# A decoder block with an RWKV-7 mixer: the order of the A products of a pair of heads on TensorE

## The chip, the cores and the metric

The kernel runs on one core of a Trainium2 chip. The metric is the device time of one execution in microseconds (us). The kernel before took 3034.74 us in the median of three runs (3031.83 to 3035.33).

The engines are named as in the profile: PE is TensorE's matmul, PEld its weight load, DVE is VectorE, ACT is ScalarE, POOL is GpSimd, SP is SyncE, which issues most DMAs.

## The reference, cut to what matters

The input x has 2048 tokens of 1024 channels. It is normalised, modulated, and multiplied by one large matrix `w_in`. The columns feed two branches: a causal depthwise convolution of width 31 with gates, and an RWKV-7 token mixer with 16 heads of 64 channels. Both are projected, merged by sigmoid gates, projected again and added to x.

The change lies in the mixer. Its state is a 64 x 64 matrix for each head, updated token by token:

```python
def step(state, inp):
    r_t, w_t, k_t, v_t, kk_t, b_t = inp
    sk = jnp.einsum('bhvk,bhk->bhv', state, kk_t)
    state = (state * w_t[:, :, None, :] - sk[..., None] * b_t[:, :, None, :]
             + v_t[..., None] * k_t[:, :, None, :])
    return state, jnp.einsum('bhvk,bhk->bhv', state, r_t)
```

## The kernel before, in words

The kernel works on this recurrence in chunks of 64 tokens. Within a chunk the tokens' influence on each other is a matrix of inner products, called A here: the products of the two operand sets `BK` (keys and in-context-rate keys, divided by their decay) and `KR` (normalised keys and receptances, multiplied by their decay). From A the kernel then inverts a triangular system and passes the state from chunk to chunk.

The 2048 tokens are four blocks (`b`) of 512, each of `NCH` = 8 chunks. In a block the 16 heads are four groups (`g`), each of two pairs (`q`), each of two heads (`hh`). So there are 4 x 4 x 2 = 32 calls of `pair`. Head 0 of a pair has its 64 channels in partitions 0 to 63 of every tile of the pair, head 1 in partitions 64 to 127.

`pair` (from line 456) prepares one pair and stops at three `yield`s. The first part makes the decay factors (the scans of line 477, the exponentials of lines 480 and 482). The second makes `KR` and `BK`: two projections through `shifted`, the eight small matmuls of line 504 for the head norms, and the element-wise lines 511, 517 (`BK`) and 522 (`KR`). The third is the place of the change:

- Lines 527 to 539, the A products. `c4` counts the two halves of the pair's eight chunks. For each half there are two PSUM tiles `pA`, one for each head, and eight matmuls (line 534): four chunks `c` and two heads `hh`, the head innermost. A matmul contracts over the head's 64 partitions and writes 128 x 128 values: chunk `c` goes to a quarter of the head's tile. The four of one head form one group in one bank (`start` at `c == 0`, `stop` at `c == 3`). Then line 537 (DVE) reads each of the two tiles, multiplies by a mask and writes `Asb`.
- Line 543 multiplies triangular parts by the norms. Lines 546 to 559 make the values (`shifted`, transposes at line 550 into a PSUM tile `pv`, and the products of lines 286 and 287 into a PSUM tile `pb`). Line 562 (POOL) overwrites `BK` in place, once all products of it are done. Line 568 transposes it, line 569 copies it out.

All those PSUM tiles have the tag `aux` and come from one pool `pa` of `PAB` = 3 buffers. A tile's first writer waits until an earlier tile has given a buffer back, that is, until its last reader is done.

After both pairs, `group` runs the inversion (POOL, lines 623 to 628, then small matmuls of lines 657 and 666) and the chain over the eight chunks: line 684 (state times operands), DVE line 686, line 689, DVE line 691, line 695, DVE line 699. That chain of a group runs while the next group's pairs are prepared. The large projections of the convolution and the gates (`conv`, `gates`, through `project` and `mm3k`, line 206) are put between all this; there are three matmuls for each tile of weights, since each 32-bit operand is split into a high and a low part.

What order results: the kernel is written for a scheduler that runs at build time. It keeps a model of the engines' time, and at each step gives an engine the instruction of highest priority (the program's order, raised in places by `tc.high_priority`) whose operands and buffers its model has ready. The result is a fixed list for each engine. On the chip each engine works through its list in order. So a matmul of head 1 whose buffer the model does not have yet is passed by others that are ready.

One `nc.tensor.matmul` on 32-bit operands stands as two records in the trace, so one half of a pair is 16 records of line 534 and a pair is 32. The projections' operands (line 206) have one record each.

Of the kernel before, what the change touches and what calls it, by code (L numbers as in the profile page):

```python
# [81 lines left out]
def hybrid_block(ctx: ExitStack, tc: tile.TileContext, x, vecs, convk, w2a2, final_g, ada, w_in, w_co, w_ro, w_o, crow, out,  # L82
                 seq=2048, groups=(0, 1, 2, 3), phase2=True, dbg=None):
    nc = tc.nc
# [48 lines left out]
    def flat(ap):  # L133
        return ap.rearrange("p a b -> p (a b)")
# [321 lines left out]
    def pair(b, q_, pr, h, lora, uv, Asb, rn, res):  # L456
# [30 lines left out]
        KR = l3.tile([P, NCH // 2, 4 * CH], F32, name="KR", tag="KR", bufs=KRB)  # L487
        BK = l3.tile([P, NCH // 2, 4 * CH], F32, name="BK", tag="BK", bufs=BKB)
# [14 lines left out]
        for c in range(NCH):  # L503
            nc.tensor.matmul(pss[prow(c % 2), c // 2, :], sq[:, c * CH:c * CH + CH], hones, start=True, stop=True,
                             skip_group_check=True)
# [20 lines left out]

        for c4 in range(NCH // 4):
            pA = [pa.tile([P, 2, 256], F32, name="aux", tag="aux") for _ in range(2)]
            for c in range(4):
                cc, e = (c4 * 4 + c) // 2, c % 2  # L530
                es = slice(e * 128, e * 128 + 128)
                for hh in range(2):
                    hs = slice(64 * hh, 64 * hh + 64)
                    nc.tensor.matmul(pA[hh][:, c // 2, es], BK[hs, cc, es], KR[hs, cc, es],  # L534
                                     start=(c == 0), stop=(c == 3), skip_group_check=True)
            for hh in range(2):
                nc.vector.tensor_tensor(  # L537
                    out=Asb[:, hh, c4 * 4:c4 * 4 + 4, :].rearrange("p (a e) n -> p a (e n)", e=2),
                    in0=pA[hh], in1=flat(maskA).unsqueeze(1).broadcast_to([P, 2, 256]), op=ALU.mult)
# [24 lines left out]
        for c4 in range(NCH // 4):  # L564
            pt = pa.tile([P, 4, P], F32, name="aux", tag="aux")
            for c in range(4):
                cc, e = (c4 * 4 + c) // 2, c % 2
# [5 lines left out]
    def group(b, g, h, lora, fill):  # L573
        uv = l3.tile([P, NCH, 2, P], F32, name="uv", tag="uv", bufs=2)
        As = [l3.tile([P, 2, NCH, P], F32, name="As", tag="As", bufs=ASB) for _ in range(2)]
        R = [{}, {}]
        rn = lt.tile([P, 2, NCH // 2, 2], F32, name="rn", tag="rn")
        pairs = [pair(b, q, 2 * g + q, h, lora, uv, As[q], rn, R[q]) for q in range(2)]
        for i, q in enumerate(ORD):
            next(pairs[q])  # L580
# [589 lines left out]
```

## Time and profile before

| what | value |
|---|---|
| median of three runs | 3034.74 us |
| the profiled execution, whole time | 3047.45 us |
| its span, first to last instruction | 3045.7 us |
| granted TensorE clock, mean over the span | 0.975 |
| stage of the four blocks' mixers (line 534 runs from 89.4 to 2309.9 us) | 2221 us |
| what follows it to the end of the span, mostly the output projections | 736 us |

The profiled execution is 12.7 us (0.4%) above the median; sums are made against it and carried over to the median as they stand.

How to read the lines: a group's line has line, engine, operation, the tile written and the tiles read, the count after x, then busy time in us and mean ns of one, then the engine's idle time just before and what ended it. A line of the timeline has the start in us, the time from the first start to the last end in us, engine, line, operation, tiles, shape, count, and in brackets the idle time before it with its releaser. A matmul's time in such a line reaches to the end of its pipeline, so the next line can start before it. A line of windows has the stretch, its length, and for each engine busy time and count, then the granted clock, the share of the DMA engines and GB/s.

### The profile page before, as it was taken

What the parts mean: (1) busy time and instruction counts of PE and PEld (TensorE: products, weight loads), DVE (VectorE), ACT (ScalarE), POOL (GpSimd) and SP (SyncE); (2) the same over time, 40 slices, a digit from 0 to 9 for tenths busy, and PEclk for the clock granted to TensorE, in tenths of its full rate; (3) what the DMA queues carried; (4) which work ended last, traced back from release to release, by engine and by line L of the source; (5) the groups of instructions that cost most, each with busy time, mean ns of one, the idle gap of its engine ahead of it and who ended that gap; (6) DMA issues with size and microseconds to landing.
All of it is one profiled execution on the core that took longest, in us unless ns stands there. A gap on an engine that the chain in (4) does not pass through costs nothing.

```text
span 3045.7 us, 64763 instructions
## 1 busy us (share of the span) xinstructions
PE 2914.9 (96%) x25672; PEld 2735.9 (90%) x25672; DVE 2058.4 (68%) x3896; ACT 935.2 (31%) x1759; POOL 1250.1 (41%) x1786
## 2 busy tenths in 40 slices
PE   6999998999999999899999999999999999899998
PEld 6889998989989899899999999999999988788988
DVE  6587877686867676668676767676779635776433
ACT  4433434332323232233232323232323222333201
POOL 3455555434343425143434263625467204565000
PEclk9899999999999999999999999999999999999999
DMA  8666758564758578847474777655647778889674
GB/s 303 205 234 209 251 196 282 199 235 145 250 185 260 187 242 287 235 137 246 151 246 139 246 254 252 199 185 165 212 141 246 229 264 309 320 311 344 239 280 163
DMA packets 368673, 699.24 MB, mean 230 GB/s; under 512 B 136241, under 2 KB 154993, under 8 KB 368370
## 3 DMA queue, kind: packets, MB, share of 16 engines
q1 hardware_dynamic: 368370, 695.10, 68.0%
q8 instruction: 202, 3.31, 0.4%
q14 instruction: 101, 0.83, 0.1%
HBM read 506.14 MB, written 187.70 MB: 228 GB/s over the span
## 4 chain that ended last, share of the span: by engine, by line
PE 61%; DMA 16%; DVE 9%; POOL 7%; SPq 3%; issue 2%; ACT 2%; ACTq 0%; DVEq 0%; POOLq 0%
PE ps_main L206 43%; DMA w_st<-w_in_t 3%; PE aux L534 2%; POOL TT L627 2%; POOL itmp L625 2%; DMA w_st<-w_ro_t 2%; DMA w_st<-w_co_t 2%; PE pout L1091 2%; PE pout L1092 2%; PE pout L1090 2%; PE xo L689 2%; DVE acc L774 1%; DMA w_gr<-grow_d 1%; PE xo L684 1%; PE xo L695 1%
## 5 line engine op out<-in xcount | busy, mean ns | idle before, releaser
L206 PE MATMUL ps_main<-h_hi,w_hi 128*128 128x256 f32 x4608 | 971.3, 289 | 12.2 <-ACT w_hi L189 3.4
L206 PE MATMUL ps_main<-h_hi,w_lo 128*128 128x256 f32 x4608 | 965.4, 289 | 8.5 <-POOL w_lo L191 5.0
L206 PE MATMUL ps_main<-h_lo,w_hi 128*128 128x256 f32 x4608 | 971.3, 289 | 0.0
L206 PEld LDWEIGHTS ps_main<-h_hi,w_hi 128*128 128x128 f32 x4608 | 735.3, 194 | 24.1 <-ACT w_hi L189 3.9
L206 PEld LDWEIGHTS ps_main<-h_hi,w_lo 128*128 128x128 f32 x4608 | 731.8, 194 | 17.5 <-POOL w_lo L191 6.3
L206 PEld LDWEIGHTS ps_main<-h_lo,w_hi 128*128 128x128 f32 x4608 | 733.9, 194 | 8.1 <-issue 0.5
L774 DVE SCALAR_TENSOR_TENSOR acc<-u,ck,acc 128x512 f32<-128x512 f32 x928 | 698.6, 753 | 20.8
L625 POOL TENSOR_TENSOR itmp<-La,TT 128x126 f32<-128x126 f32 (+22 forms) x496 | 180.2, 363 | 140.9 <-DMA La<-dA 106.1
L627 POOL TENSOR_TENSOR TT<-TT,itmp 128x126 f32<-128x126 f32 (+22 forms) x496 | 188.2, 379 | 37.3
L681 ACT ACTIVATE Se<-S,pe 128x128 f32<-128x128 f32 x256 | 89.0, 395 | 239.4 <-DVE S L699 239.2
L191 POOL TENSOR_TENSOR w_lo<-w_st,w_hi 128x1024 fp32r<-128x1024 f32 x47 | 113.6, 2417 | 112.8 <-ACT w_hi L189 106.2
L699 DVE TENSOR_TENSOR S<-xo,Se 64x128 f32<-64x128 f32 x256 | 73.5, 287 | 104.1 <-PE xo L695 100.8
L189 ACT CAST w_hi<-w_st 128x1024 fp32r<-128x1024 f32 x71 | 74.2, 1046 | 182.4 <-DMA w_st<-w_in_t 147.4
L534 PE MATMUL aux<-KR,BK 64*128 64x128 f32 x1024 | 121.5, 307 | 7.4 <-POOL BK L517 4.1
L534 PEld LDWEIGHTS aux<-KR,BK 64*128 64x128 f32 x1024 | 104.2, 208 | 18.7 <-POOL BK L517 4.3
L562 POOL TENSOR_TENSOR BK<-BK,pe 128x1024 f32<-128x1024 f32 x32 | 62.0, 1939 | 140.7 <-PE aux L534 113.1
L691 DVE TENSOR_TENSOR uv<-xo,rn 64x256 f32<-64x256 f32 x128 | 53.8, 420 | 90.7 <-PE xo L689 88.8
L686 DVE TENSOR_TENSOR XO<-xo,XO 128x256 f32<-128x256 f32 x128 | 53.7, 420 | 89.9 <-PE xo L684 70.5
L537 DVE TENSOR_TENSOR As<-aux,maskA 128x512 f32<-128x512 f32 x128 | 83.8, 685 | 36.9 <-PE aux L534 35.6
L684 PE MATMUL xo<-S,KR 128*128 128x128 f32 x512 | 83.0, 285 | 15.0 <-DVE S L699 14.9
L786 ACT ACTIVATE th<-ps_main 128x512 f32<-128x512 f32 x64 | 38.1, 596 | 190.1 <-PE ps_main L206 168.9
L431 ACT ACTIVATE t<-ps_main,mu 128x512 f32<-128x512 f32 x96 | 65.6, 683 | 97.4 <-PE ps_main L206 90.4
(301 smaller groups left out, 5318.2 us busy)
## 6 DMA issues: line engine op xcount, KB each, us to landing
w_hi<-kh_in SPq DMA_DIRECT2D x219, 512.0 KB, 5.1
w_lo<-kl_in SPq DMA_DIRECT2D x219, 512.0 KB, 4.0
w_st<-w_in_t SPq DMA_DIRECT2D x73, 512.0 KB, 4.9
kh_in<-w_hi SPq DMA_DIRECT2D x71, 512.0 KB, 2.9
kl_in<-w_lo SPq DMA_DIRECT2D x71, 512.0 KB, 3.7
w_hi<-kh_ro SPq DMA_DIRECT2D x32, 512.0 KB, 5.6
w_lo<-kl_ro SPq DMA_DIRECT2D x32, 512.0 KB, 5.5
w_hi<-kh_co SPq DMA_DIRECT2D x32, 512.0 KB, 5.5
```

Of the source, the lines that this page charges most:

```text
L189: nc.scalar.copy(hi, st)
L191: lo_eng.tensor_tensor(out=lo, in0=st, in1=hi.bitcast(F32), op=ALU.subtract)
L206: nc.tensor.matmul(ps[:, qs], ww[:, k, :], aa[k][:, qs], start=(k == 0 and t == 0 and q == 0), stop=(k == KT - 1 and t == 2 and q == ms - ...
L431: nc.scalar.activation(t1, ps, AF.Identity, scale=mu1[:, mi:mi + 1])
L534: nc.tensor.matmul(pA[hh][:, c // 2, es], BK[hs, cc, es], KR[hs, cc, es], start=(c == 0), stop=(c == 3), skip_group_check=True)
L537: nc.vector.tensor_tensor(out=Asb[:, hh, c4 * 4:c4 * 4 + 4, :].rearrange("p (a e) n -> p a (e n)", e=2), in0=pA[hh], in1=flat(maskA).unsqu ...
L625: nc.gpsimd.tensor_tensor(out=tmp[:, :ni, :nt], in0=La[:, j:j + 1, j + 1:].broadcast_to([P, ni, nt]), in1=TT[:, :ni, j:j + 1].broadcast_to ...
L627: nc.gpsimd.tensor_tensor(out=TT[:, :ni, j + 1:], in0=TT[:, :ni, j + 1:], in1=tmp[:, :ni, :nt], op=ALU.add)
L681: nc.scalar.mul(Se[:, q, :], Sg[:, q, :], R[q]["pe"][:, c:c + 1])
L684: nc.tensor.matmul(xo[:, q, :], R[q]["KR"][:, cc, es], Sg[:, q, :], start=(q == 0), stop=(q == 1), skip_group_check=True)
L699: nc.vector.tensor_tensor(out=Sg[hs, :, hs], in0=xo[hs, 2:4, hs], in1=Se[hs, :, hs], op=ALU.add)
L774: nc.vector.scalar_tensor_tensor(out=acc if i + 1 < HALO else yj, in0=u[:, i:i + TB], scalar=ck[:, j, i:i + 1], in1=acc, op0=ALU.mult, op1 ...
```

## The change

The four chunks' matmuls move into a function `aprod(c, hh)`, which is the same matmul. The first product of head 0 is issued; the first product of head 1 is to stand behind it on TensorE; all six others are to stand behind that second one. `tc.issue_after(ins)` gives every instruction traced in its block an edge of order to `ins` on the same engine; it adds no instruction and no semaphore wait of its own. The set of matmuls, their operands, tiles and flags are the same, and so are the DVE operations and the pool.

```diff
         for c4 in range(NCH // 4):
             pA = [pa.tile([P, 2, 256], F32, name="aux", tag="aux") for _ in range(2)]
-            for c in range(4):
+
+            def aprod(c, hh):
                 cc, e = (c4 * 4 + c) // 2, c % 2
                 es = slice(e * 128, e * 128 + 128)
-                for hh in range(2):
-                    hs = slice(64 * hh, 64 * hh + 64)
-                    nc.tensor.matmul(pA[hh][:, c // 2, es], BK[hs, cc, es], KR[hs, cc, es],
-                                     start=(c == 0), stop=(c == 3), skip_group_check=True)
+                hs = slice(64 * hh, 64 * hh + 64)
+                return nc.tensor.matmul(pA[hh][:, c // 2, es], BK[hs, cc, es], KR[hs, cc, es],
+                                        start=(c == 0), stop=(c == 3), skip_group_check=True)
+
+            with tc.issue_after(aprod(0, 0).ins):
+                second = aprod(0, 1)
+            with tc.issue_after(second.ins):
+                for c in range(1, 4):
+                    for hh in range(2):
+                        aprod(c, hh)
```

## The prediction

> **What bounds the kernel now.** I read the page first: which engine is full, and what the products cost. Then the windows by stage, to see whether that holds where the products lie.
>
> ```profile
> span 3045.7 us, 64763 instructions
> PE 2914.9 (96%) x25672; PEld 2735.9 (90%) x25672; DVE 2058.4 (68%) x3896; ACT 935.2 (31%) x1759; POOL 1250.1 (41%) x1786
> ...
> PE 61%; DMA 16%; DVE 9%; POOL 7%; SPq 3%; issue 2%; ACT 2%; ACTq 0%; DVEq 0%; POOLq 0%
> ...
> L774 DVE SCALAR_TENSOR_TENSOR acc<-u,ck,acc 128x512 f32<-128x512 f32 x928 | 698.6, 753 | 20.8
> ...
> L534 PE MATMUL aux<-KR,BK 64*128 64x128 f32 x1024 | 121.5, 307 | 7.4 <-POOL BK L517 4.1
> ...
> L562 POOL TENSOR_TENSOR BK<-BK,pe 128x1024 f32<-128x1024 f32 x32 | 62.0, 1939 | 140.7 <-PE aux L534 113.1
> ...
> L537 DVE TENSOR_TENSOR As<-aux,maskA 128x512 f32<-128x512 f32 x128 | 83.8, 685 | 36.9 <-PE aux L534 35.6
> ```
> ```profile
> core 0: us, PE busy (x) PEld busy (x) DVE busy (x) ACT busy (x) POOL busy (x), PEclk, DMA share, GB/s
> 89.00:114.00 25.00, 21.63 (x127) 19.49 (x128) 20.23 (x39) 13.30 (x26) 10.29 (x9) 0.60 0.56 183
> 114.00:2310.00 2196.00, 2126.31 (x20491) 2036.12 (x20489) 1573.69 (x2896) 697.97 (x1286) 982.26 (x1535) 0.98 0.65 213
> ```
>
> TensorE is full over the stage where all but the first pair's products lie: 2126.31 of 2196 us, so 69.7 us idle, while DVE is at 72%. Of TensorE's time 121.5 us are the products, 1024 records, which is 32 pairs of 32 records. A busy TensorE is not one at its peak, so the question is how densely these records stand. The timeline of one ordinary pair shows it.
>
> ```profile
> 402.18 2.05 PE L534 MATMUL aux<-KR,BK 64*128 64x128 f32 x24
> 404.16 0.50 PE L206 MATMUL ps_main<-h_lo,w_hi 128*128 128x256 f32 x2
> ...
> 406.47 1.16 PE L534 MATMUL aux<-KR,BK 64*128 64x128 f32 x8
> 407.55 0.39 PE L206 MATMUL ps_main<-h_hi,w_lo 128*128 128x256 f32 x1
> ```
> ```profile
> 402.18:403.07 0.89, 0.89 (x16) 0.89 (x17) 1.00 0.00 0
> 406.47:407.36 0.89, 0.89 (x8) 0.89 (x8) 1.00 1.01 216
> ```
>
> The run of 24 is the first half (16 records, the heads by turns) and then head 0 of the second half alone (8); the run of 8 is head 1 of the second half, later. The two windows are cut at the starts of these runs: in 0.89 us stand 16 records where the heads alternate and 8 where one head stands alone. So a record costs 0.056 us by turns and 0.112 us alone: products on the two halves of the partitions run beside each other, products on the same half do not. The second half is torn apart because its head 0 finds the third `aux` buffer free, while head 1 needs one that DVE's line 537 gives back.
>
> **The change part by part.** *First half.* By turns already; nothing changes.
>
> *Second half, head 0.* A product is 2 x 0.112 = 0.223 us alone. From 402.18 to 404.16 the long run takes 1.98 us: 0.89 for the first half, 0.89 for head 0's four products, and 0.20 that is left, for the pipeline and the change to 128-row matmuls. After the change only head 0's first product can stand there, the other three are held behind head 1's first. The run becomes 0.89 + 0.22 + 0.20 = 1.31 us: 0.67 us less.
>
> *Second half, head 1.* The later run takes 407.55 - 406.47 = 1.08 us: 0.89 for four products and 0.19 at its end. After the change it has seven products: head 1's first beside head 0's second, and so on, and head 1's last alone. That is four steps of 0.223 us again, with head 0's three hidden beside head 1's: 1.08 us as before. No run is added.
>
> The sum over the pairs is 32 x 0.67 = 21.4 us at the full clock. TensorE is what is late in this stage, and the work that follows on its list (line 206 above) moves up by as much, so most of it reaches the end.
>
> *What of it is eaten by waits.* Where TensorE already waits between these two runs for something that does not move, the gain only lengthens the wait. Two pairs of that kind:
>
> ```profile
> 1018.25 2.05 PE L534 MATMUL aux<-KR,BK 64*128 64x128 f32 x24
> ...
> 1022.26 0.68 PE L684 MATMUL xo<-S,KR 128*128 128x128 f32 x4 [1.29 <-DVE S L699]
> ```
> ```profile
> 247.19 2.05 PE L534 MATMUL aux<-KR,BK 64*128 64x128 f32 x24
> ...
> 252.00 0.81 PE L684 MATMUL xo<-S,KR 128*128 128x128 f32 x4 [2.10 <-DVE S L699]
> ```
>
> Four of the 32 pairs have such a wait of 0.4 us or more there. Those 4 x 0.67 = 2.7 us I count as nothing: 18.7 us are left.
>
> *Half clock.* Some products run at half clock and would give twice as much:
>
> ```profile
> 1159.86 0.71 PE L689 MATMUL xo<-XO,As 64*64 64x64 f32 x8 [2.25 <-DVE XO L686]
> 1160.51 3.78 PE L534 MATMUL aux<-KR,BK 64*128 64x128 f32 x24
> 1164.21 1.22 PE L695 MATMUL xo<-uv,tk 128*128 128x128 f32 x4
> ```
> ```profile
> 1160.00:1167.20 7.20, 7.20 (x46) 6.87 (x46) 2.98 (x6) 2.02 (x5) 3.81 (x4) 0.53 0.74 289
> ```
>
> Here the run takes 3.70 us, because the granted clock was 0.53 in this stretch, right behind a wait of 2.25 us. About five pairs lie so, worth up to 5 x 0.67 = 3.4 us more. I count none of it, since such stretches follow waits, and a new order may move them. One such stretch is worth 0.47 x 7.2 = 3.4 us; two more or fewer of them give +-7 us, which goes into the range.
>
> *The new wait.* Head 1's first product already waits for the buffer; now head 0's other three stand behind it, and behind them whatever TensorE's list has next. In the trace the buffer is there in time, even where DVE is late:
>
> ```profile
> 224.73 1.29 DVE L537 TENSOR_TENSOR As<-aux,maskA 128x512 f32<-128x512 f32 x2
> ```
> ```profile
> 225.63 1.16 PE L534 MATMUL aux<-KR,BK 64*128 64x128 f32 x8
> ```
>
> The first of the two ends near 224.73 + 0.68 = 225.41 us, 0.2 us ahead of head 1. This is the narrowest of the 32. In the 7.4 us that TensorE waited ahead of line 534 over the whole span, DVE's line 537 is not among the named releasers. If TensorE came there 0.67 us earlier, the stall would be 0.5 us in this pair and under 0.1 us in two others: between 0 and 0.6 us in all. I take 0: the build's model places head 1's products by the time at which its model has the buffer, and fills the place of the three products with line 206.
>
> *Behind the products.* DVE's line 537 for head 0 (0.68 us) now comes after the joint run instead of ahead of head 1's. Its `Asb` is wanted only together with head 1's, and line 562 on POOL waits for the last product, which is no later. But `aux` buffer number three comes back some 2 us later, and `pb` (line 286) wants it, at the earliest 0.4 us behind the run:
>
> ```profile
> 380.49 1.16 PE L534 MATMUL aux<-KR,BK 64*128 64x128 f32 x8
> 381.57 0.66 PE L550 MATMUL aux<-ident,vv 128*128 128x128 f32 x4
> 381.99 0.48 PE L286 MATMUL aux<-rh,bones 128*128 128x512 f32 x1
> ```
>
> Nine pairs have the transposes of line 550 right behind the run; line 286 would move by one line 537, 0 to 0.7 us each, 0 to 6 us in all. I take 0, since line 206 can stand in between, and keep 6 for the range. No DMA, DVE, ACT or POOL instruction is added or taken away.
>
> So 3047.45 - 18.7 = 3028.8 us by the profiled execution, and 3034.74 - 18.7 = 3016 us for the median.
>
> **The rivals.** *Less than it says: a third run.* If the model's list puts head 0's first product by itself, or lets steps of the chain fall between the joint products, each cut costs the end of a run:
>
> ```profile
> 563.25 0.48 PE L534 MATMUL aux<-KR,BK 64*128 64x128 f32 x2
> 563.66 0.50 PE L206 MATMUL ps_main<-h_hi,w_lo 128*128 128x256 f32 x2
> ```
>
> One product, cut off by a line 695, takes 0.41 us where 0.22 is work. A cut in each pair takes 32 x 0.19 = 6.1 us back, and the gain is 12.6: 3022 us. The Trainium skill, "TensorEngine Tiling (Array Packing)", section Key Properties, says that changing the tiling mode drains TensorE; by it each return from 64-row products to 128-row ones costs, and the 0.19 us fits. For it: several runs of the trace are cut already. Against: cuts come in the minority of pairs, and they are there before too.
>
> *No gain: the waits take it.* If the chain over the chunks (lines 684 to 699) sets the pace, TensorE only waits longer at its steps.
>
> ```profile
> PE xo L684 <- DVE S L699: 13.8, 10, 2.4
> PE xo L695 <- DVE uv L691: 11.5, 11, 2.8
> ```
>
> In all, 21 waits of 25.3 us: had each taken one pair's 0.67 us, 14 us would be gone, and 7 us left, 3027 us; with `pb` late as well (6 us) 3033 us. Against it: 28 pairs have no such wait in the right place.
>
> *Slower: the buffer blocks TensorE.* The mechanism is head 1's first product with DVE's queue behind it. If DVE reaches line 537 later than TensorE reaches that product, everything on TensorE's list stands, where before only four products of head 1 did, placed later. The price is the lateness in each of 32 places: at 0.67 us on average the gain is gone, at 1 us it is 32 x 0.33 = 10.6 us slower, 3045 us, and waits over 2 us bring half clock as at 1160 us. DVE's 928 convolution steps `acc` (line 774, 0.75 us each) in front of line 537 could do that. The Trainium skill, "TensorE: Matmul & The Clock Gate", section "Part 3: Packing small matmuls", says that matmuls start and end strictly in program order, though weight loads may run ahead. The trace agrees where line 689 waited 2.25 us (above): no matmul stands in that gap. By the rule nothing passes the blocked product. Against this rival: no such wait in the trace, where the same product waits for the same buffer.
>
> **How the numbers follow.** My forecast has 0.66, a third run 0.14, no gain 0.12, slower 0.08. The likeliest is 3016 us. Low: the whole 21.4 + 3.4 and one to two half-clock stretches fewer, 3034.74 - 24.8 - 6 = 3004. High: the third run with one or two such stretches more, 12.6 - 7 = 5 us gained, 3030; about 0.8 lie between. A difference of 0.2% (6 us) is what a measurement of this kernel can tell. Faster 0.80: the forecast and most of the third run. Same 0.12, slower 0.08.
>
> **What would show it.** The profile after should have runs of 18 and 14 records of line 534 in place of 24 and 8, of about 1.31 and 1.08 us; the group's busy time some 20 us under 121.5; no wait of line 534 on line 537; TensorE's idle time in the stage near 70 us. Wrong: waits on line 537 ahead of line 534 of over 20 us (blocked), idle time on lines 684 and 695 up by 15 us (eaten), or most pairs with three runs or more.

## The result and the profile after

The change made the kernel slower by a third of a per cent. Its median is 3043.8 us of 17 runs (3034.55 to 3049.65), against 3034.74 us of 17 runs of the kernel before (3022.09 to 3041.54): a ratio of 1.0033, 95% interval 1.0023 to 1.0043. The prediction was 3016 us.

First the page of the profile after. From line 537 on, line numbers are higher by 7: line 537 is now 544, line 562 is 569, line 684 is 691, line 695 is 702, line 699 is 706, line 774 is 781.

```profile
span 3032.8 us, 64787 instructions
PE 2871.9 (95%) x25672; PEld 2693.2 (89%) x25672; DVE 2063.8 (68%) x3896; ACT 935.8 (31%) x1759; POOL 1250.7 (41%) x1786
...
PE 46%; DMA 15%; DVE 10%; POOL 9%; issue 3%; SPq 3%; ACT 2%; POOLq 0%; DVEq 0%; ACTq 0%
...
L569 POOL TENSOR_TENSOR BK<-BK,pe 128x1024 f32<-128x1024 f32 x32 | 62.5, 1953 | 110.8 <-PE aux L534 84.6
...
L534 PE MATMUL aux<-KR,BK 64*128 64x128 f32 x1024 | 91.3, 294 | 7.9 <-POOL BK L517 3.4
L544 DVE TENSOR_TENSOR As<-aux,maskA 128x512 f32<-128x512 f32 x128 | 83.0, 684 | 19.3 <-PE aux L534 18.4
...
w_lo<-kl_in SPq DMA_DIRECT2D x219, 512.0 KB, 4.1
```

The last line is a DMA issue: these weight loads of 512 KB land 4.1 us after their issue in the median.

The products fell from 121.5 to 91.3 us, and TensorE's busy time from 2914.9 to 2871.9. But span less busy time, which is TensorE's idle time, rose from 130.8 to 160.9 us. The profiled execution itself took 3034.55 us, the lowest of the 17 runs of the change, while before's took 3047.45. So a comparison of these two profiles alone would call the change 13 us faster; the medians, not the profiled spans, carry the verdict.

The timeline of one pair in the changed kernel shows the runs:

```profile
550.18 1.38 PE L534 MATMUL aux<-KR,BK 64*128 64x128 f32 x18
551.49 0.39 PE L206 MATMUL ps_main<-h_hi,w_lo 128*128 128x256 f32 x1
...
554.38 1.16 PE L534 MATMUL aux<-KR,BK 64*128 64x128 f32 x14
555.47 0.50 PE L206 MATMUL ps_main<-h_hi,w_hi 128*128 128x256 f32 x2
```

From start to next start they take 1.31 and 1.09 us, as forecast. Not every pair looks like this. Counted over the whole timeline, line 534 stands in 93 runs, of which 18 have 18 records and 16 have 14, and 25 of the 32 pairs have three runs or more; before, it stood in 83 runs, and 18 pairs had three or more. The windows by stage and the waits of TensorE over the whole span:

```profile
114.00:2310.00 2196.00, 2103.19 (x20669) 2013.71 (x20666) 1591.78 (x2924) 705.74 (x1296) 1000.16 (x1550) 0.99 0.66 215
```
```profile
PE ps_main L206 <- DMA w_lo<-kl_in: 14.6, 2, 13.7
PE ps_main L206 <- DVE mr L1000: 13.4, 2, 11.1
PE xo L691 <- DVE S L706: 12.3, 13, 2.2
PE xo L702 <- DVE uv L698: 12.0, 12, 2.3
...
PE aux L534 <- DVE As L544: 0.4, 1, 0.4
```

TensorE is idle for 92.8 us of this stage, where it was 69.7. The steps of the chain over the chunks (lines 691 and 702) wait no longer than before (14.9 and 12.0 us over the whole span then), and the products hardly wait for the mask line. New is one wait of 13.7 us of a projection for its weights.

### The profile page after: what moved, and what is told of

It reads as the page before. It is cut to its first block, busy times and chain, and to the rows that moved or that the text cites. A ratio compares the mean times of both kernels' runs of the same rounds, so it can differ in the third digit from the quotient of the medians.

```text
span 3032.8 us, 64787 instructions
## 1 busy us (share of the span) xinstructions
PE 2871.9 (95%) x25672; PEld 2693.2 (89%) x25672; DVE 2063.8 (68%) x3896; ACT 935.8 (31%) x1759; POOL 1250.7 (41%) x1786
## 4 chain that ended last, share of the span: by engine, by line
PE 46%; DMA 15%; DVE 10%; POOL 9%; issue 3%; SPq 3%; ACT 2%; POOLq 0%; DVEq 0%; ACTq 0%
PE ps_main L206 34%; POOL TT L634 3%; POOL itmp L632 3%; DMA w_gr<-grow_d 2%; DMA La<-dA 1%; DVE acc L781 1%; DMA w_st<-w_ro_t 1%; PE xo L696 1%; DMA w_st<-w_in_t 1%; PE pout L1098 1%; PE pout L1099 1%; PE pout L1097 1%; DMA dT<-TT 1%; PE aux L534 1%; DMA xt<-x_in 1%
## 5 line engine op out<-in xcount | busy, mean ns | idle before, releaser
L206 PE MATMUL ps_main<-h_hi,w_lo 128*128 128x256 f32 x4608 | 966.9, 288 | 22.7 <-DMA w_lo<-kl_in 14.6
L206 PE MATMUL ps_main<-h_hi,w_hi 128*128 128x256 f32 x4608 | 965.1, 288 | 10.9 <-ACT w_hi L189 5.0
L534 PE MATMUL aux<-KR,BK 64*128 64x128 f32 x1024 | 91.3, 294 | 7.9 <-POOL BK L517 3.4
L696 PE MATMUL xo<-XO,As 64*64 64x64 f32 x1024 | 90.2, 227 | 5.7 <-DVE XO L693 5.6
L696 PEld LDWEIGHTS xo<-XO,As 64*64 64x64 f32 x1024 | 70.8, 136 | 27.0 <-DVE XO L693 7.9
L691 PE MATMUL xo<-S,KR 128*128 128x128 f32 x512 | 82.8, 284 | 12.3 <-DVE S L706 12.3
```

The costliest lines, as they stand in the source:

```text
L206: nc.tensor.matmul(ps[:, qs], ww[:, k, :], aa[k][:, qs], start=(k == 0 and t == 0 and q == 0), stop=(k == KT - 1 and t == 2 and q == ms - ...
L534: return nc.tensor.matmul(pA[hh][:, c // 2, es], BK[hs, cc, es], KR[hs, cc, es], start=(c == 0), stop=(c == 3), skip_group_check=True)
L691: nc.tensor.matmul(xo[:, q, :], R[q]["KR"][:, cc, es], Sg[:, q, :], start=(q == 0), stop=(q == 1), skip_group_check=True)
L696: nc.tensor.matmul(xo[pr_, q, hs], As[q][pr_, hh, c, kcol(e)], XO[pr_, c, q, hs], start=(q == 0 and hh == 0), stop=(q == 1 and hh == 1), s ...
```

## The experiments

What the source edit does to the program is seen when the two kernels' lists are laid beside each other and one counts how many instructions must be moved to make the one list out of the other. The edges concern the A products alone, but the build orders everything anew: 3,268 of 21,780 instructions are moved on TensorE, 1,051 of 3,864 on DVE, 314 of 2,308 on SP, 261 of 1,662 on ACT, 175 of 1,782 on POOL. So there were two changes in one, and two theories. The first: the products gain what was forecast, and the new order of everything else loses it again. The second: the products' gain itself doesn't reach the end. To part them, the lists were held: an edge of order from each instruction to the next on its engine, so that the build has no choice left. The kernel before ran beside all of them; ratios are to that, with the 95% interval in brackets.

**Before, held to its own lists.** The control of the method.

```diff
+        hold(tc, LISTS)
...
+            if prev is not None:
+                tc.add_manual_dep(i, prev.name, mybir.DependencyInfo(mybir.DependencyClass.NoSync, mybir.DependencyReason.DATA),
+                                  reason="hold")
+            prev = i
```

> The kernel before, with an edge of order from each instruction to the next on every engine, in the order that its own build had chosen. The program should be the one of before. Both theories: ratio 1.000 to the kernel before, within 0.1%. Its profile is a second one of the kernel before: the first stood at 3047 us, above the 17 timed runs (3022 to 3042), so this one should be nearer 3035 us.

Measured: 3033.77 us, ratio 0.9994 (0.9981 to 1.0007). Holding the lists costs nothing that can be measured, and the page, quoted for comparison with the next run, has the old price of the products.

```profile
span 3037.3 us, 64763 instructions
PE 2901.8 (96%) x25672; PEld 2722.8 (90%) x25672; DVE 2066.1 (68%) x3896; ACT 934.8 (31%) x1759; POOL 1250.6 (41%) x1786
...
L534 PE MATMUL aux<-KR,BK 64*128 64x128 f32 x1024 | 117.1, 299 | 6.4 <-POOL KR L522 3.2
```

**The old lists, products by turns.** Before's lists with one thing moved: in halves where head 0 stood alone, its three later products stand among head 1's. On DVE the mask line of the head concerned is left free to move behind the joint run. ACT, POOL and SP keep their lists exactly; 99 products are moved on TensorE, and 33 mask operations are free on DVE. The list edit of one pair:

```diff
 L206 MATMUL ps_main<-h_lo,w_hi 128x256 x2
-L534 MATMUL aux<-KR,BK 128x128 x12
+L534 MATMUL aux<-KR,BK 128x128 x9
 L684 MATMUL xo<-S_421,KR 128x128
...
-L534 MATMUL aux<-KR,BK 128x128 x4
+L534 MATMUL aux<-KR,BK 128x128 x7
 L550 MATMUL aux<-ident,vv 128x128 x4
```

> The lists of before on all engines, with one edit: the three later products of head 0 in the second half are moved behind head 1's first, by turns with head 1's (and in the first pair's first half too), and DVE's mask of that head is free to follow them. Theory A, the new lists: the products by turns save some 20 us by themselves, and the change lost that and 9 us more because the build ordered everything else anew. Then this is 15 to 25 us faster than before, ratio 0.992 to 0.995. Theory B, the products: holding head 0 back costs by itself (TensorE blocked at the buffer, the third buffer back later). Then this is slower than before, ratio 1.002 to 1.005, as the change was.

Measured: 3019.17 us against 3036.94, ratio 0.9945 (0.9929 to 0.9960): 17.8 us faster by the medians, where the prediction had 18.7. Its page, and two of TensorE's waits:

```profile
span 3017.7 us, 64767 instructions
PE 2876.3 (95%) x25672; PEld 2699.2 (89%) x25672; DVE 2059.6 (68%) x3896; ACT 934.7 (31%) x1759; POOL 1253.8 (42%) x1786
...
L534 PE MATMUL aux<-KR,BK 64*128 64x128 f32 x1024 | 89.6, 299 | 8.6 <-POOL BK L517 4.1
```
```profile
PE aux L286 <- DVE As L537: 2.0, 3, 1.7
...
PE aux L534 <- DVE As L537: 0.4, 1, 0.4
```

Against the control's page 27.5 us of products went and 19.6 us of span, while TensorE's idle time (span less busy time) rose from 135.5 to 141.4 us; the mask line holds the products up for 0.4 us and line 286, behind them, for 2.0 us. The first theory stands for its first half. This kernel is faster than both the kernel before and the change.

**The change once more.** The changed kernel as it is, on the same chip as the two above and the one below.

```diff
+            with tc.issue_after(aprod(0, 0).ins):
+                second = aprod(0, 1)
+            with tc.issue_after(second.ins):
```

> The changed kernel once more, on the chip of the other three, with another profile. Both theories: ratio to before 1.002 to 1.004. Its first profile stood at 3034.6 us, the lowest of 17 runs; this one should be nearer 3044 us, and the difference between the two profiles shows where executions of one program differ.

Measured: 3044.66 us, ratio 1.0021 (1.0005 to 1.0037), so the loss repeats. The profiled execution, 3034.12 us, is again at the low end of its runs (3033.64 to 3057.12).

**The new lists, products head by head.** The changed kernel held to its lists, but from head 1's first product on head 1's four stand ahead of head 0's three.

```diff
-L534 MATMUL aux_1306<-KR_1137,BK_1138 128x128
-L534 MATMUL aux_1305<-KR_1137,BK_1138 128x128
-L534 MATMUL aux_1306<-KR_1137,BK_1138 128x128
-L534 MATMUL aux_1305<-KR_1137,BK_1138 128x128
-L534 MATMUL aux_1306<-KR_1137,BK_1138 128x128
-L534 MATMUL aux_1305<-KR_1137,BK_1138 128x128
-L534 MATMUL aux_1306<-KR_1137,BK_1138 128x128
+L534 MATMUL aux_1306<-KR_1137,BK_1138 128x128 x4
+L534 MATMUL aux_1305<-KR_1137,BK_1138 128x128 x3
```

> The lists of the changed kernel on all engines, with one edit: in the later run of the second half, head 1's four products stand ahead of head 0's three instead of by turns with them. Nothing else moves. Theory A: 32 runs become 3 products of 0.22 us longer, 21 us in all; ratio to before about 1.010, to the changed kernel about 1.007. Theory B, that products by turns bring nothing at the end of the kernel: as the changed kernel, ratio to before 1.003.

Measured: 3049.02 us, ratio 1.0045 (1.0026 to 1.0064): 4.4 us over the change run beside it by the medians, 7 by the ratios, with some 7 either way. The two profiles are 15.4 us apart, and line 534 is busy for this long:

```profile
L534 PE MATMUL aux<-KR,BK 64*128 64x128 f32 x1024 | 105.1, 294 | 6.5 <-POOL BK L517 2.7
```

That is 13.7 us more than in the repeat of the change (91.4), not 21. The expectation was too high: it charged three products of 0.22 us to each of 32 runs. Both kernels have the same 93 runs, and only 16 of them are full ones of 14 records. A full one shows what the other order costs, in the timeline and in the window of its first 0.89 us:

```profile
557.44 1.49 PE L534 MATMUL aux<-KR,BK 64*128 64x128 f32 x14
558.86 0.51 PE L206 MATMUL ps_main<-h_hi,w_hi 128*128 128x256 f32 x2
```
```profile
557.44:558.33 0.89, 0.89 (x11) 0.89 (x12) 1.00 0.86 249
```

It takes 1.42 us from start to next start, 0.33 us more than by turns, where 0.67 was expected. Eleven records start in the first 0.89 us, where one head alone has 8, so head 0's first products still stand beside head 1's last ones. Whether more was lost to waits can't be told within 7 us.

**Where in the span the new lists lose.** The next kernels follow one set of lists up to a point and the other from there on; what the first set had not issued yet follows in the second's order. All have the products by turns; `mix(X, k, Y)` in the diffs is list X to its k-th matmul of line 206, then Y. "Old" is the list of the second experiment, "new" that of the change. The points are counted in matmuls of line 206. In the traces of these kernels the 6500th starts near 1175 us, the 7200th near 1290 and the 13500th near 2350, behind the stage of the mixers; the expectations put them at 1190, 1330 and 2380 us.

New to the 6500th, then old:

```diff
-LISTS = old
+LISTS = mix(new, 6500, old)
```

> Products by turns throughout. The changed kernel's lists up to the 6500th projection matmul (about 1190 us, near the end of block 1), from there on the old lists with the products by turns (those of the second kernel of this study, 0.9945). Theory A1, the new lists lose in the second part alone: by the profiles they are some 15 us ahead at this place, so this is faster than 0.9945: 3004 to 3015 us, ratio 0.990 to 0.993. Theory A2, the loss is spread over all the lists: about half of the 25 us between the two, ratio 0.998.

Measured: 3027.1 us, ratio 0.9948 (0.9932 to 0.9964), as the old lists throughout and between the two forecasts. Within the intervals, the new order loses nothing in this part and brings nothing extra.

Old to the 6500th, then new:

```diff
-LISTS = old
+LISTS = mix(old, 6500, new)
```

> The other half: the old lists with the products by turns up to the 6500th projection matmul, the changed kernel's lists from there. Theory A1: all of the loss and more, ratio 1.004 to 1.008 to before. Theory A2: half of the loss, ratio 0.998.

Measured: 3050.62 us, ratio 1.0034 (1.0019 to 1.0049). Within the intervals, all the loss lies behind the 6500th matmul.

Old to the 7200th, then new:

```diff
-LISTS = mix(old, 6500, new)
+LISTS = mix(old, 7200, new)
```

> As the run before, but the old lists go on to the 7200th projection matmul (about 1330 us), past the boundary from block 1 to block 2, where TensorE waits 14 to 16 us in one piece for a weight load in the profiles of the changed lists (9 us in three pieces in the old ones). If that boundary is the place of the loss, this is 6 us or more faster than the run before, ratio about 0.998 to 1.002; if the loss lies behind it, the two are the same within 3 us.

Measured: 3040.32 us, ratio 0.9997 (0.9983 to 1.0012), on the same chip as the one above and 10.3 us faster. So the 115 us or so in which the second block of tokens gives way to the third cost some 11 us.

New to the 13500th, then old:

```diff
-LISTS = new
+LISTS = mix(new, 13500, old)
```

> The changed kernel's lists up to the 13500th projection matmul (about 2380 us, the end of the mixer's stage), then the old lists for the output stage. By the profiles the new lists lose 9 us in the output stage: then this is 3035 us, ratio 0.999 to before and 0.997 to the changed kernel. If the output stage is innocent: as the changed kernel, 1.002 to 1.003.

Measured: 3043.94 us, ratio 1.0004 (0.9994 to 1.0013), between the two expectations: 0.0017 to 0.0029, some 5 to 9 us, under the change.

Old to the 13500th, then new:

```diff
-LISTS = old
+LISTS = mix(old, 13500, new)
```

> The old lists with the products by turns up to the 13500th projection matmul (about 2380 us), the changed kernel's lists for the output stage alone. If the output stage's new lists lose 5 to 9 us by themselves: ratio to before 0.9962 to 0.9975. If they lose nothing: 0.9945, and the rest of the loss is all in blocks 2 and 3.

Measured: 3033.63 us, ratio 0.9975 (0.9959 to 0.9991). The new order of the output stage costs 0.0030, some 9 us. These are TensorE's waits from 2380 us on, first with the old lists throughout, then with the new ones from there:

```profile
PE ps_main L206 <- DVE mr L993: 13.2, 4, 8.2
PE pout L1091 <- DMA w_lo<-kl_o: 1.7, 1, 1.7
```
```profile
PE ps_main L206 <- DVE mr L993: 14.6, 2, 11.2
PE pout L1091 <- DMA w_lo<-kl_o: 6.1, 2, 4.6
```

5.8 us more are waited for the merged input and for output weights. The windows from 2520 to 2640 us in the same order show another part, the granted clock (third from the end):

```profile
2520.00:2640.00 120.00, 107.01 (x646) 93.41 (x644) 74.45 (x149) 43.34 (x88) 64.87 (x48) 0.97 0.90 330
```
```profile
2520.00:2640.00 120.00, 104.21 (x627) 92.08 (x626) 77.41 (x159) 42.19 (x86) 63.10 (x47) 0.93 0.87 312
```

By a rough estimate, 0.04 of 120 us is 4.8 us of clock.

| stretch with the new lists in place of the old | from | cost |
|---|---|---|
| to the 6500th matmul, near 1175 us | 0.9948 - 0.9945 | 1 us |
| 6500th to 7200th, near 1175 to 1290 us | 1.0034 - 0.9997 | 11 us |
| 7200th to 13500th, near 1290 to 2350 us | 0.9997 - 0.9975 | 7 us |
| from the 13500th, near 2350 us | 0.9975 - 0.9945 | 9 us |

Each difference is uncertain by some 6.5 us (two intervals of 4.5 us, put together), so the 7 us are barely told from nothing. Only in the second row do both kernels come from one chip, and what the change-over from one list to another costs by itself was not measured. Added to 0.9945, the first three rows give 1.0007 for new lists up to the output stage, where that kernel measured 1.0004.

**The block's end by itself.** Here is the timeline of TensorE in the changed kernel, and then that of SP's queue just before:

```profile
1228.59 0.40 PE L206 MATMUL ps_main<-h_lo,w_hi 128*128 128x256 f32 x2
1242.65 0.79 PE L206 MATMUL ps_main<-h_hi,w_lo 128*128 128x256 f32 x2 [13.66 <-DMA w_lo<-kl_in]
1243.24 0.63 PE L206 MATMUL ps_main<-h_hi,w_hi 128*128 128x256 f32 x2
```
```profile
1216.35 11.95 SPq L645 DMA_DIRECT2D As<-dT  x16
1228.40 0.38 SPq L883 DMA_DIRECT2D grow_d<-hgate_col  x1
1228.83 0.58 SPq L764 DMA_DIRECT2D ro_d<-th  x1
1229.51 0.38 SPq L183 DMA_DIRECT2D w_lo<-kl_in  x1
```

Line 883 writes a column of 1024 gate values, 4 KB in pieces of 4 bytes, to memory, and the weights that TensorE waits for are issued 1.1 us behind it. The DMA view of this stretch, with time to landing last, and the windows, with clock, DMA share and GB/s last:

```profile
w_lo<-kl_in SPq DMA_DIRECT2D x4, 512.0 KB, 10.2
...
grow_d<-hgate_col SPq DMA_DIRECT2D x1, 4.0 KB, 10.9
```
```profile
1232.00:1236.00 4.00, 0.00 (x0) 0.00 (x0) 2.38 (x7) 0.00 (x0) 0.00 (x0) 0.52 0.34 26
1236.00:1240.00 4.00, 0.00 (x0) 0.00 (x0) 0.00 (x0) 0.00 (x0) 0.00 (x0) 0.50 0.26 31
```

While the column is on its way, the DMA engines move 26 to 31 GB/s. With the old lists (the second experiment) the same write stands behind the weights, as the timelines of SP's queue and of TensorE show:

```profile
1219.23 10.63 SPq L638 DMA_DIRECT2D As<-dT  x16
...
1230.44 0.38 SPq L183 DMA_DIRECT2D w_lo<-kl_in  x1
...
1240.31 0.37 SPq L876 DMA_DIRECT2D grow_d<-hgate_col  x1
```
```profile
1234.64 0.80 PE L206 MATMUL ps_main<-h_hi,w_lo 128*128 128x256 f32 x2 [2.79 <-DMA w_lo<-kl_in]
```

So the next kernel is the change held to its lists, with this one write moved behind the next six weight loads; nothing else differs.

```diff
 L645 DMA As<-dT 32x4x32 x16
-L883 DMA grow_d<-hgate_col 128x8x1
 L764 DMA ro_d_7_146<-th 128x512
...
 L182 DMA w_hi<-kh_in_531 128x1024
+L883 DMA grow_d<-hgate_col 128x8x1
 L794 DMA gc_d_7_242<-th 128x512
```

> The changed kernel's lists with one DMA moved on SP's list: the write of the gate column (grow_d<-hgate_col, 4 KB in pieces of 4 bytes) goes behind the next six weight loads instead of standing one place ahead of the first of them. Theory C, that write is what the 14 us wait at the block boundary is made of (it takes 11 us to land, at about 30 GB/s, and the weight load behind it 13 us): the wait falls to 5 us or less and the kernel is 8 to 11 us faster than the change, ratio to before 0.999 to 1.000. Theory D, the 16 small copies into As ahead of both are what delays the load: the wait stays at 10 us or more, ratio 1.002 to 1.003.

Measured: 3043.5 us, ratio 1.0003 (0.9987 to 1.0018). Its timeline of TensorE:

```profile
1236.08 0.79 PE L206 MATMUL ps_main<-h_hi,w_lo 128*128 128x256 f32 x2 [5.41 <-DMA w_lo<-kl_in]
...
1255.28 0.80 PE L206 MATMUL ps_main<-h_hi,w_hi 128*128 128x256 f32 x2 [6.03 <-ACT h_hi L362]
```

The long wait falls from 13.66 to 5.41 us, which shows that the column's place makes most of its length. But another of 6.03 us comes 20 us later, for the next block's input, so only 2.2 us of waiting are gone. SP's queue and the windows of this kernel show where the column now stands:

```profile
1236.74 0.37 SPq L883 DMA_DIRECT2D grow_d<-hgate_col  x1
...
1240.67 0.65 SPq L371 DMA_DIRECT2D hf<-xT  x1
```
```profile
1244.00:1248.00 4.00, 4.00 (x35) 4.00 (x35) 1.65 (x4) 0.00 (x0) 0.00 (x0) 1.00 1.58 57
1248.00:1252.00 4.00, 1.26 (x11) 1.05 (x9) 0.00 (x0) 0.00 (x0) 0.00 (x0) 1.00 0.84 46
```

It is ahead of a load of that input, which lands 13.9 us after its issue, while the DMA engines move 46 to 57 GB/s. So the column seems to have passed its delay on to the next load that TensorE needs; no run moves it behind that load too.

The ratio is 0.0018 below the repeat of the change and 0.0030 below the first measurement, 5 to 9 us, with intervals that overlap.

**Another build with the same products.** The edges only in the second half of each pair, where the products were apart; the build orders the whole program anew once more.

```diff
-            with tc.issue_after(aprod(0, 0).ins):
-                second = aprod(0, 1)
-            with tc.issue_after(second.ins):
+            first, second = aprod(0, 0), aprod(0, 1)
+            held = [tc.issue_after(second.ins)] if c4 else []
+            with ExitStack() as stack:
+                for h_ in held:
+                    stack.enter_context(h_)
                 for c in range(1, 4):
```

> A source edit, lists left to the build: the six later products are held behind head 1's first only where c4 is 1; in the first half, which was by turns before, there are no edges. The products stand nearly as in the change, but the build orders everything else once more. If the build's order is a matter of chance of some 10 us or more, this can land anywhere from 3010 to 3050 us, and not within 3 us of the change; theory B (the products themselves cost) says 1.003 as the change.

Measured: 3034.78 us, ratio 0.9965 (0.9950 to 0.9980). The group of the products in its page:

```profile
L534 PE MATMUL aux<-KR,BK 64*128 64x128 f32 x1024 | 95.1, 301 | 14.1 <-POOL KR L522 9.0
```

The products are no cheaper than in the change (95.1 against 91.3 us, with more waiting ahead of them), yet the kernel is faster than the change by 0.0056 to 0.0068, some 17 to 21 us. What differs is the order of the rest. Among TensorE's waits there is a long one at the block's end here too, for the next input. From 1190 to 1330 us all its waits come to 15.9 us, against 18.9 in the change, so little of this build's lead comes from there:

```profile
PE ps_main L206 <- DMA hf<-xT: 11.0, 1, 11.0
```

## Why the prediction was wrong

Right, by the prediction's own steps:

- *The price of a record, by turns and alone.* The runs of 18 and 14 records take 1.31 and 1.09 us. The products' busy time fell by 30.2 us between the profiles before and after, and by 27.5 between the control and the old lists by turns.
- *The sum, in part by luck.* 18.7 us were forecast; with everything but the mask line held, the products by turns brought 17.8. Two errors nearly cancel in this. The products gave 27.5 us by the two pages and not 21.4: "no run is added" misses that nine runs are gone (74 in place of 83), and the half clock was left out; how the surplus divides is not shown. And more than 2.7 us of it was lost: TensorE's idle time rose by 5.9 us between these pages.
- *The new wait.* It was bounded by 0 and 0.6 us and taken at 0. It is 0.4 us in the waits after, and 0.4 with the old lists. `pb` (line 286), for which 0 to 6 us were kept, waits 2.0 us there.
- *The rivals.* The buffer doesn't block TensorE, and the chain's waits don't lengthen (12.3 and 12.0 us against 14.9 and 12.0). A third run came in part: 93 runs in place of 83, ten cuts of 0.19 us, 1.9 us by estimate, or 3.6 us against the 74 runs of the old lists by turns. None of the three makes the change slower than before.

Two readings were wrong without deciding anything. Cuts do not come "in the minority of pairs": 18 of the 32 had three runs or more before, so the sign "most pairs with three runs or more", which did come (25 of 32), could not tell the rivals apart. And waits over 2 us do not always bring half clock "as at 1160 us": in the profile before, the granted clock in the 3.4 us behind waits of 2.38 us (at 629.5 us) and 2.77 us (at 1005.0 us) is 1.00, where it is 0.55 behind the 2.25 us at 1160.

The step that failed is this one: "the work that follows on its list moves up by as much, so most of it reaches the end." The sentence takes it for granted that there is a list that follows and stays. The build makes the list, and with the edges it made another one for all engines. The prediction knew this ("the build's model ... fills the place of the three products with line 206") and allowed +-7 us for it, as half-clock stretches more or fewer. The new order cost 25 us by the repeat of the change on the same chip (3044.66 - 3019.17), 27 by the ratios of the pieces: 11 us where the second block gives way to the third, 9 in the output stage, 7 between. Less 17.8, that is 8 to 9 us slower than before; measured are 6 to 10. Only the second figure is a check, since it uses no time of the change itself (it is 1.0034 - 0.9945). One sign that the prediction named says the same: TensorE's idle time in the stage is 92.8 us, not near 70.

The rule of the Trainium skill that was weighed, "TensorE: Matmul & The Clock Gate", section "Part 3: Packing small matmuls", that matmuls run strictly in program order, agrees with these traces, but the product that it was to hold up was not late. It applies to the block's end instead: while the projection waits 13.66 us for its weights, no matmul stands in the gap.

For the block's end the mechanism is shown in part: with the column's write ahead of the weights the wait is 13.7, 15.6, 14.3, 14.6 and 14.1 us in the five profiles that have this order, and with the write behind them 2.8 and 5.4 in the two shown. The Trainium skill, "DMA: Bandwidth & Descriptors", section "Rules for kernel authors", says that a non-contiguous last dimension is moved as one descriptor for each element; the 10.9 us for 4 KB and the 26 GB/s fit. That the time of the whole kernel falls by 11 us with this wait is not shown, since part of the waiting moved to the next input. In the output stage the lost time is located in two waits and in the clock, but nothing there was changed by itself.

What stays open: which instructions cost the 7 us between the 7200th and the 13500th matmul, if they are there; whether the column's write would cost nothing behind the input's loads as well; and why both profiled executions of the change lie some 10 us below its median, so that no profile shows a typical run of it.

## What to carry to other kernels

Where a build orders the program, one edge of order is a change of all engines' lists: price the edit by itself, and then give the new order a range that is as wide as a second build with the same edit shows (here 0.9965 and 1.0021 to 1.0033). To know what an edit is worth, hold all other instructions to the old lists and move only what it concerns; here that version is also the fastest of all, 3019.17 us. And look in the new lists for what now stands ahead of the loads that the full engine needs next.

## What the runs showed of the hardware

A write of 4 KB in pieces of 4 bytes took 10.9 us to land. A load of 512 KB issued 1.1 us behind it on the same queue held TensorE up for 13.66 us, where such a load lands in 4.1 us in the median. The granted clock was 0.50 to 0.52 in that gap, and the first matmuls behind it ran at the lower rate (0.63 us for two where it was 0.40). With the write moved behind six weight loads, the wait was 5.41 us, and an input load issued 3.9 us behind the write landed after 13.9 us.
